# Grouping the output stores of an attention-times-value kernel in pairs, and putting SyncE's relay words into a register loop

## Chip, cores, metric

One core of one Trainium2 chip. The metric is the device time of one execution in microseconds (us). All runs told here were undisturbed ("fast"), so they are compared directly. "Ratio" is the mean time of one kernel's fast runs over that of the other's fast runs of the same rounds on the same chip, so it is not quite the ratio of the medians that are quoted.

In the profile's lines PE is TensorE's matrix multiply and PEld its weight load, DVE is VectorE, ACT ScalarE, POOL GpSimd and SP SyncE; a q behind a name means the engine's sequencer. HBM is the memory off the core, SBUF the one on it, and PSUM (in "banks") takes PE's results. A landing is the moment at which a transfer by DMA is complete.

## The reference

```python
batch, n_heads, seq, head_dim = 8, 12, 1024, 64
# attn_weights: (8, 12, 1024, 1024) float32;  v: (8, 12, 1024, 64) float32
out = np.einsum('bhqs,bhsd->bhqd', attn_weights, v).astype(np.float32)
```

The weights are 402.65 MB, v and the output 25.17 MB each.

## The kernel before

The 96 heads are taken in 24 quads of four heads; a quad is two units of 8.39 MB of weights. GpSimd loads each unit (float32 in HBM, bf16 in SBUF) into one of two buffers. PE transposes a unit's 16 groups, which frees its buffer, and multiplies with v; VectorE and ScalarE empty PSUM; ScalarE writes results to `osb`, a ring of ten quad slots, from which they are stored.

GpSimd's steady program: when the transposes of unit n are done, the load of unit n + 2 is issued; ahead of it, at odd quads, the next v load; behind it, at even quads, one store of eight heads (2.10 MB).

```python
for n in range(NU - 2):                      # NU = 48 units, NV = 24 quads
    q, i = n // 2, n % 2
    if i == 0 and q % 2 == 1 and q + 1 < NV:
        ...                                  # waits for the old v's last use
        load_v((q + 1) // 2)
    pool.wait_ge(s_t[True], (n + 1) * PER_DVE)
    load_attn(n + 2)
    if i == 0 and q % 2 == 0 and 0 < q <= HELD_FROM:    # HELD_FROM = 16
        store_2(q - 2)
for q in range(HELD_FROM, BY_SYNC, 2):       # held back to the end: quads 16 to 19
    store_2(q)
```

SyncE turns DMA completions into words (semaphore increments) for the engines: `s_half` for each landed unit, `s_vr` for each v, `s_free` for each stored pair of slots. PE waits for `s_half` at the ninth of a unit's 16 groups; ScalarE waits for `s_free` before it writes a slot again.

```python
for n in range(-2, NU - 2):                  # straight-line, one wait and one increment each
    if n + 2 < HALVED:
        nc.sync.wait_ge(s_abf[n % 2], 16 * ((n + 2) // 2 + 1))
    else:
        nc.sync.wait_ge(s_second[n + 2], 16)
    nc.sync.sem_inc(s_half)
    if n >= 0 and n % 2 == 0:
        q = n // 2
        if q % 2 == 1 and q + 1 < NV:
            nc.sync.wait_ge(s_v, 16 * ((q + 1) // 2))
            nc.sync.sem_inc(s_vr, 2)
        if q % 2 == 1 and 1 < q <= HELD_FROM:
            nc.sync.wait_ge(s_osb[(q - 3) // 2 % 2], 16 * ((q - 3) // 4 + 1))
            nc.sync.sem_inc(s_free)
# ... then the last stores, issued by SyncE
```

Of the kernel before, what the change touches and what calls it, by code (L numbers as in the profile page):

```python
# [10 lines left out]
def kernel(  # L11
# [18 lines left out]
    nc = tc.nc  # L30
# [15 lines left out]
    VB = S // VP // SB  # L46
    NV = NH // VH
    NU = 2 * NV


    HELD_FROM = NV - 8
# [4 lines left out]

    HALVED = NU - 2

    def slot(q):
        return q % NO  # L60
# [20 lines left out]
    with tc.tile_critical(no_gpsimd_drain=True):  # L81
# [18 lines left out]
        s_abf = [sem(f"s_abf{i}") for i in range(2)]  # L100
        s_second = {n: sem(f"s_second{n}") for n in range(HALVED, NU)}
        s_v0, s_v = sem("s_v0"), sem("s_v")
        s_osb = [sem(f"s_osb{i}") for i in range(2)]
# [13 lines left out]
        s_memset, s_const, s_vr = sem("s_memset"), sem("s_const"), sem("s_vr")  # L117

        s_half, s_free = sem("s_half"), sem("s_free")
# [33 lines left out]
        def transpose_back(parts=((0, 4, px[0]), (4, 4, px[1]))):  # L153
            for j0, jn, ps in parts:
                for j in range(jn):
                    last = pe.matmul(  # L156
                        out=ps[:, ds(j * P, P)],
                        lhsT=ot[:, j0 + j],
                        rhs=ident,
                        is_transpose=True,  # L160
                        start=(j == 0),
                        stop=(j == jn - 1),
                    )
                last.then_inc(s_back)
# [16 lines left out]
        def wait_both(s, n):  # L181
            for x in s:
                pe.wait_ge(x, n)

        def pe_unit(i, n, loaded, it):

            pe.wait_ge(*loaded)
            for g in range(G):
                if g == GH:
                    pe.wait_ge(s_half, n)  # L190
                transpose_g(abf[i], g, n)
            wait_both(s_ot, n)
            if i == 0:
                pe.wait_ge(s_vr, it)
                odd = pe.snap((it - 1) % 2)
                with pe.If(odd > 0):
                    spread_v(1, po + px)
                with pe.Else():
                    spread_v(0, po + px)
                wait_both(s_vbf, it * 2)  # L200
            transpose_back()
            wait_both(s_last, n)
            for hp in range(2):
                for h in range(2):
                    for half in range(2):
                        outs = po[hp][ds(half * D, D), ds(h * GH * VP, GH * VP)]
                        last = multiply(outs, 2 * hp + h, half)
                last.then_inc(s_m[hp])

        pe.wait_ge(s_const, 1 + VH)  # L210
        with nc.Fori(1, NV + 1, 1, engines=(PE,)) as it:
# [4 lines left out]
            pe_unit(1, second, (s_abf[1], loaded), it)  # L216
        wait_both(s_ot, NU + 1)
        transpose_back()


        def engine(dve):
# [11 lines left out]
            def back_copy(rows, j0, jn, ps, count):  # L233

                eng.wait_ge(s_back, count)
                return copy(  # L236
                    out=rows.rearrange("p (half j) d -> p j half d", half=2)[:, ds(j0, jn)],
                    in_=ps[:, ds(0, jn * P)].rearrange("p (j half d) -> p j half d", half=2, d=D),
                )
# [59 lines left out]
            rows = osb[:, slot(NV - 1), ds(G, G)]  # L299
            back_copy(rows, 4 * k, 4, px[k], 2 * NU + k + 1).then_inc(s_fin[k])  # L300

# [13 lines left out]
        def load_attn(n):  # L315
            pieces = [(0, G)] if n < HALVED else [(0, GH), (GH, GH)]
            for g0, gn in pieces:
                pool.dma_start(  # L318
                    out=abf[n % 2][:, ds(g0, gn)].rearrange("p g s -> p (g s)"),
                    in_=attn_q[n // 2][:, ds((n % 2 * G + g0) * S, gn * S)],  # L320
                ).then_inc(s_abf[n % 2] if g0 == 0 else s_second[n], 16)

        def load_v(iv):
            pool.dma_start(  # L324
                out=vr.rearrange("p two b x -> p two (b x)"), in_=v_2[iv]
            ).then_inc(s_v, 16)

        def store(q, fours, eng, done):
            eng.wait_ge(s_out, 2 * (q + fours) + 1)
            at_slot = osb[:, ds(slot(q), fours)].rearrange("p n r d -> p n (r d)")  # L330
            eng.dma_start(  # L331
                out=out_2[q // 2] if fours == 2 else out_q[q],
                in_=at_slot if fours == 2 else at_slot[:, 0],
                **({"single_packet": True} if eng is pool else {}),
            ).then_inc(done, 16)

        def store_2(q):
            store(q, 2, pool, s_osb[q // 2 % 2] if q < HELD_FROM else s_held)
# [14 lines left out]
        for h in range(VH):  # L353
# [9 lines left out]
            ).then_inc(s_const)  # L363
        for n in range(NU - 2):
            q, i = n // 2, n % 2
            if i == 0 and q % 2 == 1 and q + 1 < NV:
                for s in s_sp:
                    pool.wait_ge(s, 2 * q + 2)
                load_v((q + 1) // 2)
            pool.wait_ge(s_t[True], (n + 1) * PER_DVE)  # L370
            load_attn(n + 2)
            if i == 0 and q % 2 == 0 and 0 < q <= HELD_FROM:
                store_2(q - 2)
        for q in range(HELD_FROM, BY_SYNC, 2):
            store_2(q)
# [9 lines left out]
                out=v32_2[ds(p0, pn), two], in_=v_2[0][ds(p0, pn), two]  # L385
            ).then_inc(s_v0, 16)
        nc.sync.sem_inc(s_free, RING)
        for n in range(-2, NU - 2):

            if n + 2 < HALVED:  # L390
                nc.sync.wait_ge(s_abf[n % 2], 16 * ((n + 2) // 2 + 1))
            else:
                nc.sync.wait_ge(s_second[n + 2], 16)
            nc.sync.sem_inc(s_half)
            if n >= 0 and n % 2 == 0:
                q = n // 2
                if q % 2 == 1 and q + 1 < NV:
                    nc.sync.wait_ge(s_v, 16 * ((q + 1) // 2))
                    nc.sync.sem_inc(s_vr, 2)
                if q % 2 == 1 and 1 < q <= HELD_FROM:  # L400
                    nc.sync.wait_ge(s_osb[(q - 3) // 2 % 2], 16 * ((q - 3) // 4 + 1))
                    nc.sync.sem_inc(s_free)
        store(NV - 4, 2, nc.sync, s_end)
        store(NV - 2, 1, nc.sync, s_end)
        rows = osb[:, slot(NV - 1)].rearrange("p (u half j) d -> p u half j d", u=2, half=2)
# [41 lines left out]
```

## Time and profile before

| | before |
|---|---|
| median of the first 3 runs | 1054.85 us (1054.56 to 1054.9) |
| span of the profiled run | 1053.1 us |
| PE / ACT / DVE busy | 70 / 39 / 37% |
| share of the DMA engines, queue q0 | 99.1% |
| HBM traffic | 427.82 MB read, 25.17 MB written |

The row of the page that shows the stores one by one is the rate in 40 slices of 26 us, in GB/s, in the page's table of slices. It counts bytes on the SBUF side, where a load of weights is halved by the cast (4096 KB in the page's list of issues for the 8.39 MB of a unit) and a store is not (2048 KB, 2.10 MB), so a slice with a store in it stands out:

```profile
GB/s 235 224 217 218 218 244 219 219 214 249 231 214 251 215 219 258 217 219 230 243 217 210 259 217 218 259 219 219 248 217 217 218 211 225 219 208 230 206 216 339
```

The slices near 218 hold loads alone; those near 250 hold a store of 2.10 MB, and the last one is the burst of held stores.

### The profile page before, as it was taken

The numbers are of one execution on the slowest core, as the hardware profiler recorded it, in microseconds if no ns is written. First come the engines' busy times: TensorE is split into PE (matmuls) and PEld (weight loads), VectorE is DVE, ScalarE is ACT, GpSimd is POOL, SyncE is SP. The second block draws the span as 40 slices with busy tenths as digits, with TensorE's granted clock in tenths as the row PEclk, the third lists the DMA queues.
The fourth block names the chain that finished last, engine by engine and source line by source line (L and its number), as shares of the span: only waits on it lengthen the run. The fifth ranks groups of instructions, "written<-read, shape, count | busy, mean of one in ns | idle before, by whom it ended". The sixth has DMA issues, their size and how long they took to land.

```text
span 1053.1 us, 16530 instructions
## 1 busy us (share of the span) xinstructions
PE 738.0 (70%) x6920; PEld 692.4 (66%) x6920; DVE 388.8 (37%) x582; ACT 410.3 (39%) x493; POOL 45.1 (4%) x80
## 2 busy tenths in 40 slices
PE   0787677676697568667768757765776866875885
PEld 0686676565686567656668657765766866865874
DVE  0453343333353234333334324433333433532542
ACT  0354344433353334333335334433333533533542
POOL 1000000000000000000000000000000000000000
PEclk9989888898798888889879888888887987988998
DMA  9999999999999999999999999999999999999998
GB/s 235 224 217 218 218 244 219 219 214 249 231 214 251 215 219 258 217 219 230 243 217 210 259 217 218 259 219 219 248 217 217 218 211 225 219 208 230 206 216 339
DMA packets 14330, 240.19 MB, mean 228 GB/s; under 512 B 1269, under 2 KB 1781, under 8 KB 4725
## 3 DMA queue, kind: packets, MB, share of 16 engines
q0 software_dynamic: 12912, 233.84, 99.1%
q1 hardware_dynamic: 1413, 6.29, 1.5%
q8 instruction: 2, 0.03, 0.0%
q14 instruction: 3, 0.02, 0.0%
HBM read 427.82 MB, written 25.17 MB: 430 GB/s over the span
## 4 chain that ended last, share of the span: by engine, by line
DMA 75%; PE 22%; issue 1%; DVE 0%; SPq 0%; ACT 0%; POOL 0%; DVEq 0%
DMA abf<-in_attn_weights_dram 72%; PE bank L129 21%; DMA osb<-in_v_dram 3%; PE bank L171 1%; PE bank L156 0%; DVE vbf L229 0%; SPq L384 0%; PE bank L144 0%; DVE at L250 0%; DVE osb L236 0%; ACT ot L262 0%; POOL abf L318 0%; DVEq L249 0%; DVE vr L308 0%; DVEq L283 0%
## 5 line engine op out<-in xcount | busy, mean ns | idle before, releaser
L129 PE MATMUL bank<-ident,abf 128*128 128x128 f32 x3072 | 454.1, 318 | 273.6 <-DMA abf<-in_attn_weights_dram 264.4
L129 PEld LDWEIGHTS bank<-ident,abf 128*128 128x128 f32 x3072 | 444.2, 214 | 286.8 <-DMA abf<-in_attn_weights_dram 276.2
L250 DVE COPY at<-bank 128x1024 bf16<-128x1024 bf16 x480 | 320.4, 689 | 463.8 <-PE bank L129 460.0
L250 ACT COPY at<-bank 128x1024 bf16<-128x1024 bf16 x288 | 288.8, 1012 | 419.9 <-PE bank L129 419.9
L171 PE MATMUL bank<-at,vbf 128*64 128x256 bf16 x3072 | 215.0, 278 | 0.0
L171 PEld LDWEIGHTS bank<-at,vbf 128*64 128x64 bf16 x3072 | 196.8, 108 | 13.4 <-DVE at L250 4.0
L262 ACT COPY ot<-bank 128x512 f32<-128x512 f32 x48 | 28.1, 586 | 174.2 <-PE bank L171 174.2
L262 DVE COPY ot<-bank 128x512 f32<-128x512 f32 x48 | 33.2, 692 | 151.3 <-PE bank L171 151.3
L156 PE MATMUL bank<-ident,ot 128*128 128x128 f32 x392 | 52.2, 276 | 32.9 <-DVE vbf L229 32.1
L156 PEld LDWEIGHTS bank<-ident,ot 128*128 128x128 f32 x392 | 43.4, 141 | 45.0 <-DVE vbf L229 43.9
L236 ACT COPY osb<-bank 128x512 f32 (+1 forms) x97 | 52.2, 589 | 27.1 <-PE bank L156 26.3
L318 POOL DMA_DIRECT2D abf<-in_attn_weights_dram x50 | 27.3, 546 | 692.4 <-PE bank L129 691.4
L229 DVE CAST vbf<-bank 128x512 bf16<-128x512 f32 x48 | 30.9, 686 | 6.5 <-PE bank L144 6.5
L229 ACT CAST vbf<-bank 128x512 bf16<-128x512 f32 x48 | 25.8, 589 | 11.8 <-PE bank L144 11.8
L144 PE MATMUL bank<-vr,spread 32*128 32x512 bf16 x384 | 25.8, 377 | 0.0
L324 POOL DMA_DIRECT2D vr<-in_v_dram x11 | 7.8, 706 | 234.9 <-PE bank L144 234.9
L250 ACT ACT_TABLE_LOAD x12 | 15.4, 1283 | 1.3 <-SPq L81 1.1
L144 PEld LDWEIGHTS bank<-vr,spread 32*128 32x128 bf16 x384 | 10.2, 92 | 6.7
L308 DVE CAST vr<-osb 128x4096 bf16<-128x4096 f32 x1 | 2.3, 2294 | 30.4 <-DMA osb<-in_v_dram 30.4
L331 POOL DMA_DIRECT2D out_dram<-osb x10 | 7.2, 717 | 30.4 <-ACT osb L236 30.4
L355 POOL TENSOR_SCALAR_AFFINE_SELECT spread<-spread 32x512 bf16<-32x512 bf16 x4 | 2.5, 631 | 0.6
L236 DVE COPY osb<-bank 128x512 f32<-128x512 f32 x1 | 0.7, 692 | 3.1 <-PE bank L156 3.1
(8 smaller groups left out, 2.1 us busy)
## 6 DMA issues: line engine op xcount, KB each, us to landing
abf<-in_attn_weights_dram POOLq DMA_DIRECT2D x46, 4096.0 KB, 33.3
out_dram<-osb POOLq DMA_DIRECT2D x10, 2048.0 KB, 29.5
vr<-in_v_dram POOLq DMA_DIRECT2D x11, 1024.0 KB, 17.2
abf<-in_attn_weights_dram POOLq DMA_DIRECT2D x4, 2048.0 KB, 24.4
out_dram<-osb SPq DMA_DIRECT2D x1, 2048.0 KB, 13.7
osb<-in_v_dram SPq DMA_DIRECT2D x1, 1024.0 KB
out_dram<-osb SPq DMA_DIRECT2D x1, 1024.0 KB, 15.8
osb<-in_v_dram SPq DMA_DIRECT2D x1, 768.0 KB
```

What stands on the lines that cost most here:

```text
L129: last = pe.matmul(out=pt[g % 4][:, k], lhsT=words[:, k], rhs=ident, is_transpose=True, start=(k == 0), stop=(k == KW - 1),)
L144: last = pe.matmul(out=ps, lhsT=spread[rows, b], rhs=vr[rows, two, b], start=(b == 0), stop=(b == VB - 1),)
L156: last = pe.matmul(out=ps[:, ds(j * P, P)], lhsT=ot[:, j0 + j], rhs=ident, is_transpose=True, start=(j == 0), stop=(j == jn - 1),)
L171: last = pe.matmul(out=outs, lhsT=vbf[:, 2 * kw + par, h], rhs=at[:, ds(half * GH, GH), kw, ds(h * VP, VP), par], start=(n == 0), stop=(n ...
L229: copy(out=vbf[:, :, h], in_=ps.rearrange("p (k d) -> p k d", k=SB)).then_inc(s_vbf[e])
L236: return copy(out=rows.rearrange("p (half j) d -> p j half d", half=2)[:, ds(j0, jn)], in_=ps[:, ds(0, jn * P)].rearrange("p (j half d) -> ...
L250: ins = copy(out=at[:, g].rearrange("c k j two -> c (k j two)"), in_=bank[g % 4].bitcast(bf16),)
L262: copy(out=ot.rearrange("c j (h p) -> c h j p", h=VH)[:, ds(2 * e, 2)], in_=po[e].rearrange("c (h j p) -> c h j p", h=2, j=GH),).then_inc( ...
L318: pool.dma_start(out=abf[n % 2][:, ds(g0, gn)].rearrange("p g s -> p (g s)"), in_=attn_q[n // 2][:, ds((n % 2 * G + g0) * S, gn * S)],).th ...
L324: pool.dma_start(out=vr.rearrange("p two b x -> p two (b x)"), in_=v_2[iv]).then_inc(s_v, 16)
L331: eng.dma_start(out=out_2[q // 2] if fours == 2 else out_q[q], in_=at_slot if fours == 2 else at_slot[:, 0], **({"single_packet": True} if ...
L355: pool.affine_select(out=spread[ds(h * VP, VP)], in_=spread[ds(h * VP, VP)], compare_op=mybir.AluOpType.not_equal, fill=1.0, base=0, patte ...
```

## The change

The intent: fewer turns between loading and storing, by issuing two stores of eight heads together at every sixteenth head, and a shorter program for SyncE, by a register loop whose turn covers sixteen heads.

```diff
-            if i == 0 and q % 2 == 0 and 0 < q <= HELD_FROM:
+            if i == 0 and q % 4 == 0 and 0 < q <= HELD_FROM:
+                store_2(q - 4)
                 store_2(q - 2)
...
-        for n in range(-2, NU - 2):
-            (the straight-line words, shown above)
+        def relay(to, of, n, by=1):
+            nc.sync.wait_ge(of, n)
+            nc.sync.sem_inc(to, by)
+        def relays_of(four, eight, stored):
+            for n in range(4):
+                relay(s_half, s_abf[n % 2], four + 16 * (2 + n // 2))
+                if n == 2:
+                    relay(s_vr, s_v, eight + 16, 2)
+                    if stored is not None:
+                        nc.sync.wait_ge(s_osb[0], stored)
+                        relay(s_free, s_osb[1], stored, 2)
+        for i in range(2):
+            relay(s_half, s_abf[i], 16)
+        for t in range(2):
+            relays_of(32 * t, 16 * t, None)
+        with nc.Fori(1, HELD_FROM // 4 + 1, 1, engines=(mybir.EngineType.SP,)) as it:
+            stored = nc.sync.snap(it * 16)
+            for k in range(2):
+                four, eight = (nc.sync.snap(it * (2 * x) + k * x) for x in (32, 16))
+                relays_of(four, eight, stored if k == 0 else None)
+        for t in range(HELD_FROM // 2 + 2, NV // 2 - 1):
+            relays_of(32 * t, 16 * t, None)
+        for n in range(HALVED, NU):
+            relay(s_half, s_second[n], 16)
```

(The dots and the bracketed line mark cuts.)

More of the change, by code (lines that the diff above doesn't have):

```diff
@@ L387 @@
         nc.sync.sem_inc(s_free, RING)
-        for n in range(-2, NU - 2):
-            if n + 2 < HALVED:
-                nc.sync.wait_ge(s_abf[n % 2], 16 * ((n + 2) // 2 + 1))
-            else:
-                nc.sync.wait_ge(s_second[n + 2], 16)
-            nc.sync.sem_inc(s_half)
-            if n >= 0 and n % 2 == 0:
-                q = n // 2
-                if q % 2 == 1 and q + 1 < NV:
-                    nc.sync.wait_ge(s_v, 16 * ((q + 1) // 2))
-                    nc.sync.sem_inc(s_vr, 2)
-                if q % 2 == 1 and 1 < q <= HELD_FROM:
-                    nc.sync.wait_ge(s_osb[(q - 3) // 2 % 2], 16 * ((q - 3) // 4 + 1))
-                    nc.sync.sem_inc(s_free)
+        def relay(to, of, n, by=1):
[22 more added lines that the diff above has]
+            relay(s_half, s_second[n], 16)
         store(NV - 4, 2, nc.sync, s_end)
```

## The prediction

> **What bounds the kernel now.** I read the page's header and its table of slices first, then the queues and the bytes, then the chain of work that ended last in order of time, then a table of four stretches, and last the waits of GpSimd and SyncE.
>
> ```profile
> PE 738.0 (70%) x6920; PEld 692.4 (66%) x6920; DVE 388.8 (37%) x582; ACT 410.3 (39%) x493; POOL 45.1 (4%) x80
> DMA  9999999999999999999999999999999999999998
> q0 software_dynamic: 12912, 233.84, 99.1%
> q1 hardware_dynamic: 1413, 6.29, 1.5%
> q8 instruction: 2, 0.03, 0.0%
> q14 instruction: 3, 0.02, 0.0%
> HBM read 427.82 MB, written 25.17 MB: 430 GB/s over the span
> ```
>
> No compute engine is above 70%, while the 16 DMA engines are full in every slice. HBM traffic, 427.82 + 25.17 = 452.99 MB, is just the inputs (402.65 MB of weights, 25.17 of v) and the output (25.17), each once. So no byte can be saved. Instruction fetches on q8 and q14 are five packets in all.
>
> The chain of waits in order of time gives the pace of the stream. Its columns are start, length and what; every PE row is the start of an odd half-quad's transposes, the moment its load has landed, so two neighbouring PE starts are two loads of 8.39 MB apart, plus what lay between them in the queue:
>
> ```profile
> 436.30 10.42 PE bank L129 x64
> ...
> 479.81 8.03 PE bank L129 x64
> ...
> 523.35 9.67 PE bank L129 x64
> ...
> 566.89 9.46 PE bank L129 x64
> ...
> 828.58 8.03 PE bank L129 x64
> 836.61 0.28 issue
> 836.89 30.29 DMA abf<-in_attn_weights_dram
> 867.23 9.49 PE bank L129 x64
> ```
>
> The table of stretches (columns: length, then PE, weight load, DVE, ACT and POOL busy, PE clock, DMA share, GB/s counted at the SBUF side) has a period with one store, one with one v load, and one with neither:
>
> ```profile
> 479.81:523.35 43.54, 29.61 (x288) 27.74 (x288) 15.94 (x24) 16.41 (x20) 1.81 (x3) 0.89 1.00 237
> 523.35:566.89 43.54, 30.94 (x288) 29.06 (x288) 15.94 (x24) 17.72 (x21) 1.78 (x3) 0.84 1.03 220
> 828.58:867.23 38.65, 29.38 (x289) 27.50 (x289) 15.94 (x24) 16.41 (x20) 1.79 (x3) 0.91 0.98 210
> ```
>
> The bare period moves 16.78 MB in 38.65 us: 434 GB/s. A store of eight heads (2.10 MB) adds 43.54 - 38.65 = 4.89 us, which is 429 GB/s; a v load of the same HBM bytes adds the same 4.89 us. So a store costs its bytes and nearly nothing else. The chain itself calls only 72% DMA on the weights and 21% PE, because it goes from a landing back to the issue and from there to the transposes that freed the buffer. That is not what paces the stream: an issue joins a queue that still holds the other buffer's load.
>
> ```profile
> POOL abf L318 <- PE bank L129: 691.4, 35, 37.4
> POOL out_dram L331 <- ACT osb L236: 30.4, 8, 3.8
> SPq L394 <- DMA abf<-in_attn_weights_dram: 1025.7, 48, 25.2
> ```
>
> GpSimd waits 3.8 us before each of the eight stores, after the load has been issued. SyncE spends 1025.7 of 1053.1 us waiting for loads.
>
> [...]
>
> **The change part by part.** (1) Stores. GpSimd issued eight stores of eight heads in the steady part, one every second quad (a quad is four heads, two loads): at quads 2, 4, ... 16, each behind a load. Now it issues none at quads 2, 6, 10, 14 and two at 4, 8, 12, 16. The count stays at eight, the bytes too, and the shape (256 rows of 8 KB) too. First-order cost: 8 x 4.89 = 39.1 us before and after, difference 0. A period holding a pair should become 38.65 + 2 x 4.89 = 48.4 us and its counterpart without one 38.65; two such together are 87.1, the same as 2 x 43.54.
>
> What could be gained is a cost of switching between loads and a store. I bound it by the chain: the eight periods with a store (130.23 to 174.51, 218.05 to 262.02 and so on) last 44.28, 43.97, 43.64, 43.59, 43.54, 43.73, 43.83 and 43.57 us, mean 43.77; those with a v load 43.50 to 43.54, mean 43.52. The excess is 0.25 us each, 2.0 us in total. It is uneven, and the least of them has 0.02, so it need not belong to the stores. If all of it went with the switch, half the switches would save 1.0 us. I give this one chance in two: -0.5 us.
>
> The first store of a pair finds its rows written long ago, so GpSimd no longer waits 3.8 us before it; the second still does. That wait lay behind an issued load and is worth 0. Issuing the two takes 2 x 0.71 us of GpSimd, against over 10 us until it is wanted again. 0.
>
> (2) Free slots. The ring has ten quad slots. A slot pair used to be handed back when the load after its store had landed, at quads 3, 5, ...; now two come at once at quads 5, 9, 13, 17. ScalarE's sixth turn (quads 10 and 11) needs the sixth word, its eighth (14 and 15) the eighth; these come at quads 5 and 9. There are about five quads, over 200 us, to spare. 0.
>
> (3) SyncE's words. Every landing is still followed by one wait and one increment, now with thresholds in registers, plus some register operations and a branch in four turns. PE asks for the word of a load only at its ninth group, halfway through transposes of 8 to 10 us, so some 4 us after landing. [...] Even if PE did wait, the stream would not: by the chain it frees a buffer and GpSimd issues 8 to 11 us after a landing, and the next load (38.65 / 2 = 19.3 us) then still runs for about 9 us. [...]
>
> (4) Start and end. The first loads, the held stores of quads 16 to 19 and the last stores from SyncE are untouched. 452.99 MB at 434 GB/s are 1043.6 us of the 1053.1; the 9.5 us left are start, end and unevenness, outside the change. 0.
>
> Sum: 1054.85 - 0.5 - 0.05 = 1054.3 us.
>
> **The rivals.** *A dearer pair:* four megabytes of writes in a row could slow the memory or make a load late[...]. For it speaks only that no two stores are queued together before the very end. Against it: the issue that must not be late has 9 us to spare, growing by another store's 4.9 us, and at the end stores already run back to back. At 0.5 us for each pair this is +2 us, 1056.9.
>
> *Switching is what costs:* the whole 0.25 us excess goes with a switch, and perhaps the loads behind it become smoother: -1.0 to -2.0 us, 1052.9 to 1053.9. For it: only store periods have an excess above 0.02 us. Against: it does not repeat from one store to the next.
>
> *The register loop stalls SyncE:* [...] PE would then stand at its ninth group, and waits of PE for SyncE would appear. With 9 us of slack the time does not move; only a stall over 9 us each turn would give +1 to +10 us. I take it as very unlikely.
>
> *Nothing is to be had:* the store pieces are hidden work in a saturated stream and both parts are housekeeping: 1054.8.
>
> **Range and chances.** The runs before spread over 0.34 us. The rivals that I give weight reach from 1052.9 to 1056.9, the upper one with less. Predicted 1054.3 us, range 1052.9 to 1055.7 for 8 in 10. A 2% step is 21 us, more than ten times every term above: faster 0.01, same 0.98, slower 0.01.
>
> **What would show it.** Right: the same bytes, the DMA row full, the chain's periods cycling 48.4 / 43.5 / 38.65 / 43.5 us in the steady part with the same sum of about 174 us for eight loads, and GpSimd's waits before stores down from eight to four of 3.8 us. The switching cost: a pair's period below 48.4 + 0.25. A stalled SyncE: waits of PE or PEld on SyncE at line 129 beyond the two (5.4 us) there now at the halved loads. Wrong altogether: a slice with DMA below 9 in the steady part, GpSimd waiting at a DMA issue, ScalarE waiting for a free slot, or a bare period other than 38.6 us.

The sum, 1054.3 us, still counts a term of -0.05 us: it was the guess at what a shorter program for SyncE saves. The term that is left, the switching's, gives 1054.85 - 0.5 = 1054.35 us. A time for the bookkeeping of a loop's turn, also a guess, was never in the sum.

## The result, and the profile after

| | before | after |
|---|---|---|
| median of 6 runs each | 1054.8 us (1053.95 to 1055.22) | 1054.12 us (1053.7 to 1055.15) |
| ratio after / before | | 0.9996, 95% interval 0.9983 to 1.0009 |
| span of the profiled run | 1053.1 us | 1052.8 us |

The same time within noise. The medians differ by 0.7 us; the interval is 1.4 us wide to either side. The page of the changed kernel:

```profile
PE 727.1 (69%) x6920; PEld 681.4 (65%) x6920; DVE 388.3 (37%) x582; ACT 410.1 (39%) x493; POOL 44.9 (4%) x80
DMA  9999999999999999999999999999999999999998
GB/s 236 223 220 209 218 213 218 218 260 245 230 217 204 221 218 296 219 219 218 219 209 212 300 217 219 218 219 219 287 216 218 217 211 225 219 207 231 204 217 337
...
q0 software_dynamic: 12912, 233.84, 99.0%
...
q14 instruction: 2, 0.02, 0.0%
HBM read 427.82 MB, written 25.17 MB: 430 GB/s over the span
```

The stores did move: a single store's peak near 250 is gone, and four groups appear, the first cut by a slice's edge (260 and 245), then 296, 300 and 287. The bytes are the same and the DMA row is as full as before. The one other difference in the queues is an instruction packet on q14, 2 for 3. PE's 11 us less of busy time are no gain: PE is idle for loads anyway, and its waits for them rose from 264.4 to 278.2 us.

The stretches between PE's starts on odd units, the table that the prediction reads, for four neighbouring periods of the changed kernel (columns: length, busy time of PE, weight load, DVE, ACT and POOL, PE clock, DMA share, GB/s):

```profile
386.77:435.43 48.66, 29.37 (x288) 27.50 (x289) 15.94 (x24) 16.40 (x20) 1.81 (x3) 0.84 0.99 254
435.43:478.97 43.54, 32.12 (x288) 30.25 (x288) 16.13 (x24) 17.73 (x21) 1.07 (x2) 0.82 1.04 222
478.97:517.62 38.65, 29.39 (x288) 27.51 (x289) 15.94 (x24) 16.41 (x20) 1.78 (x3) 0.91 0.98 211
517.62:561.16 43.54, 29.74 (x288) 27.87 (x289) 15.94 (x24) 17.68 (x21) 2.48 (x4) 0.88 1.04 222
```

A period with a pair of stores, one with a v load, a bare one, one with a v load: 48.66, 43.54, 38.65, 43.54, together 174.39 us. Before, two store periods and two v periods took 2 x 43.54 + 2 x 43.54 = 174.2 us where the store periods were at their best. The time for a store has moved from one period into another, and that is all.

The waits, and SyncE's own:

```profile
POOL out_dram L332 <- ACT osb L237: 12.4, 4, 3.1
PE bank L130 <- SPq L393: 3.9, 2, 3.3
```

```profile
SPq L393 <- DMA abf<-in_attn_weights_dram: 1021.9, 48, 29.4
```

GpSimd now waits four times before a store instead of eight. PE waits for SyncE only at the two halved loads of the end, as before. SyncE itself does little but wait for loads.

### The profile page after: what moved, and what is told of

It reads as the page before. It is cut to its first block, busy times and chain, and to the rows that moved or that the text cites. A ratio compares the mean times of both kernels' runs of the same rounds, so it can differ in the third digit from the quotient of the medians.

```text
span 1052.8 us, 16564 instructions
## 1 busy us (share of the span) xinstructions
PE 727.1 (69%) x6920; PEld 681.4 (65%) x6920; DVE 388.3 (37%) x582; ACT 410.1 (39%) x493; POOL 44.9 (4%) x80
## 4 chain that ended last, share of the span: by engine, by line
DMA 76%; PE 21%; issue 1%; DVE 0%; SPq 0%; ACT 0%; POOL 0%; DVEq 0%
DMA abf<-in_attn_weights_dram 74%; PE bank L130 20%; DMA osb<-in_v_dram 3%; PE bank L172 1%; PE bank L157 0%; DVE vbf L230 0%; SPq L386 0%; PE bank L145 0%; DVE at L251 0%; DVE osb L237 0%; ACT ot L263 0%; POOL abf L319 0%; DVEq L250 0%; DVE vr L309 0%; DVEq L284 0%
## 5 line engine op out<-in xcount | busy, mean ns | idle before, releaser
L130 PE MATMUL bank<-ident,abf 128*128 128x128 f32 x3072 | 443.3, 314 | 283.6 <-DMA abf<-in_attn_weights_dram 278.2
L130 PEld LDWEIGHTS bank<-ident,abf 128*128 128x128 f32 x3072 | 433.4, 214 | 296.8 <-DMA abf<-in_attn_weights_dram 290.1
L263 ACT COPY ot<-bank 128x512 f32<-128x512 f32 x48 | 28.1, 586 | 174.2 <-PE bank L172 174.2
```

The source lines that it names most:

```text
L130: last = pe.matmul(out=pt[g % 4][:, k], lhsT=words[:, k], rhs=ident, is_transpose=True, start=(k == 0), stop=(k == KW - 1),)
L263: copy(out=ot.rearrange("c j (h p) -> c h j p", h=VH)[:, ds(2 * e, 2)], in_=po[e].rearrange("c (h j p) -> c h j p", h=2, j=GH),).then_inc( ...
```

## The experiments

The theory: the DMA stream is full from start to end, a store costs its bytes wherever it stands, and SyncE's words have slack. The rivals: a switch between loads and stores costs, so that grouping pays; or the register loop stalls SyncE. Two lengths are used for all runs. The **stream** is the time from the landing of unit 3 to that of unit 45, and the **end** that from the landing of unit 47, the last, to the end of the span. They come from the trace's landing records (one for each of the 16 DMA engines; the landing is the last of them). Landings and PE's starts agree within about 0.05 us in the steady part.

### The two kernels again

No edit.

> The kernel before, unedited, for a second trace. Theory (a saturated stream, the grouping of stores is worth nothing): ratio 1.000, and the uneven excess of the store periods (0.02 to 0.77 us in the first trace) falls on other periods or vanishes, as it is no property of the stores. Rival (a switch between loads and a store costs): the eight store periods again exceed the v-load periods by about 0.25 us in the mean, largest at the first ones.

> The changed kernel, unedited. Theory: ratio to before 0.9995 to 1.0005, a difference below 0.5 us. Rival (switching cost saved): 0.998 to 0.999, 1 to 2 us faster. In its first trace a period with a pair of stores lasted 48.7 to 48.8 us against 38.65 + 2 x 4.89 = 48.4; if that is the pair's own cost it repeats here.

Measured: before again 1054.62 us, ratio 1.000 (0.9986 to 1.0014); after again 1054.13 us, ratio 0.9995 (0.9981 to 1.0008). The chain of waits of the kernel before, second trace (start, length, what):

```profile
129.96 9.49 PE bank L129 x64
...
174.04 10.11 PE bank L129 x64
...
217.58 8.03 PE bank L129 x64
...
261.14 9.30 PE bank L129 x64
```

The store periods here are 44.08 (129.96 to 174.04) and 43.56 us (217.58 to 261.14); in the first trace the same two were 44.28 and 43.97. All eight of this trace have a mean of 43.75, against 43.77 in the first. So the rival's half of the expectation came true: the excess of some 0.2 us stays with the store periods and did not wander off to others. But its parts are scattered, from 0.02 to 0.54 us here. In the changed kernel the pair periods were 48.58 to 48.67 us in the second trace and 48.66 to 48.78 in the first, 0.15 to 0.35 above 38.65 + 2 x 4.89 = 48.43.

### Each half of the change alone

Paired stores with straight-line words:

```diff
-            if i == 0 and q % 2 == 0 and 0 < q <= HELD_FROM:
+            if i == 0 and q % 4 == 0 and 0 < q <= HELD_FROM:
+                store_2(q - 4)
                 store_2(q - 2)
...
-                if q % 2 == 1 and 1 < q <= HELD_FROM:
-                    nc.sync.wait_ge(s_osb[(q - 3) // 2 % 2], 16 * ((q - 3) // 4 + 1))
-                    nc.sync.sem_inc(s_free)
+                if q % 4 == 1 and 1 < q <= HELD_FROM + 1:
+                    for k in range(2):
+                        nc.sync.wait_ge(s_osb[k], 16 * (q // 4))
+                    nc.sync.sem_inc(s_free, 2)
```

> The paired stores alone, SyncE's words straight-line as before. Theory: ratio 0.9995 to 1.0005. Rival switching cost: as fast as the whole change, 0.998 to 0.999. Rival loop: if the register loop were what moved the time, this one stays at 1.000 and the loop alone moves.

The register loop with single stores (from the changed kernel):

```diff
-            if i == 0 and q % 4 == 0 and 0 < q <= HELD_FROM:
-                store_2(q - 4)
+            if i == 0 and q % 2 == 0 and 0 < q <= HELD_FROM:
                 store_2(q - 2)
...
-        with nc.Fori(1, HELD_FROM // 4 + 1, 1, engines=(mybir.EngineType.SP,)) as it:
-            stored = nc.sync.snap(it * 16)
+        with nc.Fori(1, HELD_FROM // 4, 1, engines=(mybir.EngineType.SP,)) as it:
+            stored = [(s_osb[1], nc.sync.snap(it * 16)), (s_osb[0], nc.sync.snap(it * 16 + 16))]
...
```

(The words of a turn are changed to match: one free slot pair at a time, and three turns instead of four.)

> The register loop alone (three turns), single stores as before. Theory: ratio 0.9995 to 1.0005, words sent within 0.1 us of the landing, no wait of PE on SyncE beyond the two at the halved loads. Rival[...]: waits of several us at line 129's PE rows in three turns, and 1.001 to 1.01.

Measured: pairs alone 1054.47 us, ratio 1.000 (0.9987 to 1.0014), with pair periods of 48.43 to 48.68 us; loop alone 1054.74 us, ratio 1.000 (0.9986 to 1.0013). The loop alone leaves this in the waits of PE, and this in the queues:

```profile
PE bank L130 <- SPq L392: 4.0, 2, 2.0
```

```profile
q14 instruction: 2, 0.02, 0.0%
```

Two waits, those of the halved loads: the loop stalls nobody. And the page answers which half removed the instruction packet: the loop. The five profiled kernels with this loop as it stands (the change twice, the loop alone and the two last experiments) have 2 packets on q14, the six with straight-line words have 3. These counts are of the span. In the trace of the loop alone an 8 KB packet begins 0.4 us after the span's end and another 1.3 us after it, where the straight-line kernels have just one, some 1.2 us after: there the packet slid past the end and was not saved. In both traces of the whole change it is gone. One packet of 8 KB, which took 0.31 us in the first trace of before, is the most that the shorter program bought.

### Larger and smaller groups

Four stores together at every 32nd head, and one store of four heads at every quad, both with straight-line words:

```diff
-            if i == 0 and q % 2 == 0 and 0 < q <= HELD_FROM:
-                store_2(q - 2)
+            if i == 0 and q % 8 == 0 and 0 < q <= HELD_FROM:      # fours
+                for x in (8, 6, 4, 2):
+                    store_2(q - x)
+            if i == 0 and 0 < q <= HELD_FROM:                      # or: halves
+                store(q - 1, 1, pool, s_osb[(q - 1) // 2 % 2])
```

(SyncE's thresholds for free slots are changed to match.)

> Four stores of eight heads back to back at every 32nd head (two groups in place of eight single stores), words straight-line. Theory: bytes alone count, ratio 0.9995 to 1.0005, a period with four stores lasts 38.65 + 4 x 4.89 = 58.2 us (up to 59 if each back-to-back store costs 0.1 us more, as the pairs seemed to). Rival switching cost: a quarter of the switches, 0.997 to 0.9985, 1.5 to 3 us faster.

> Sixteen stores of four heads, one per quad, in place of eight of eight heads: twice the switches, the same bytes. Theory: ratio 0.9995 to 1.001 (each period 38.65 + 2.45 = 41.1 us, plus the v load in every second one). Rival switching cost of 0.25 us or more each: 1.002, 2 us or more slower.

Measured: fours 1055.37 us, ratio 1.0004 (0.9991 to 1.0018); halves 1055.0 us, ratio 1.0003 (0.9989 to 1.0017). The stretch of the fours with the first group:

```profile
376.77:435.46 58.69, 29.80 (x288) 27.91 (x288) 15.99 (x24) 16.40 (x20) 1.81 (x3) 0.79 0.99 283
```

and two neighbouring stretches of the halves:

```profile
349.71:395.70 45.99, 31.38 (x288) 29.50 (x288) 16.04 (x24) 17.73 (x21) 1.60 (x3) 0.82 1.03 232
395.70:436.83 41.13, 31.74 (x288) 29.87 (x288) 16.13 (x24) 16.45 (x20) 2.32 (x4) 0.88 0.99 225
```

Four stores add 58.69 - 38.65 = 20.04 us, 5.01 each. A store of half the size and a v load add 45.99 - 38.65 = 7.34 us, just 4.89 + 4.89 / 2; in the next stretch a half-size store alone adds 2.48, against 2.45. So twice the switches cost no more, and a quarter of them save nothing that these runs resolve. The rival "a switch costs 0.25 us" wanted 1.5 to 3 us less for the fours and 2 us or more for the halves; neither came.

### No steady stores

The eight stores, SyncE's wait for each and the last wait for all of them are left out; SyncE hands the slots back unconditionally. The output of the first 16 quads is wrong.

```diff
-            if i == 0 and q % 2 == 0 and 0 < q <= HELD_FROM:
-                store_2(q - 2)
...
-                    nc.sync.wait_ge(s_osb[(q - 3) // 2 % 2], 16 * ((q - 3) // 4 + 1))
                     nc.sync.sem_inc(s_free)
```

> The eight steady stores left out; the output of the first 16 quads is wrong on purpose. Theory (a store costs its bytes in a full stream): 8 x 4.89 = 39.1 us less, 1015.7 us, ratio 0.963. Rival (stores partly hidden beside the loads): clearly less gain, for instance 20 us. Rival (stores cost their switches too): 41 us or more.

Measured: 1014.54 us, ratio 0.9617 (0.9602 to 0.9632); 40.2 us less than the 1054.72 of before in the same rounds, 5.02 us for each store. Two stretches:

```profile
296.63:335.26 38.63, 29.81 (x289) 27.94 (x289) 15.96 (x24) 16.41 (x20) 1.78 (x3) 0.91 0.97 208
335.26:378.80 43.54, 30.11 (x288) 28.25 (x289) 16.04 (x24) 17.67 (x21) 1.06 (x2) 0.84 1.05 225
```

Nothing of a store is hidden beside the loads: taking it away gives its whole time back. And with no store in the stream every period is 38.62 to 38.67 or 43.52 to 43.56 us, without a single one of the irregular longer ones. So the excess, 0.05 to 0.3 us for a store in the mean (table below), does belong to the stores, but by the halves and fours not to the number of switches.

### Late words

From the changed kernel, an idle count in SyncE between a load's landing and the word to PE:

```diff
             nc.sync.wait_ge(of, n)
+            if to is s_half:
+                with nc.Fori(0, 20, 1, engines=(mybir.EngineType.SP,)):     # 65 in the second
+                    nc.sync.sem_inc(s_idle)
             nc.sync.sem_inc(to, by)
```

> The changed kernel with about 6 us of idle counting in SyncE ahead of each word to PE. Theory (9 us of slack in the issue): PE waits about 2 us on SyncE in each of 46 more loads, and the time stays within 1 us, ratio 0.999 to 1.001. Rival (what PE waits goes to the end): 46 x 2 = 92 us slower, 1.09.

> The changed kernel with about 20 us of idle counting ahead of each word to PE, past the slack. Theory: a buffer is freed 20 + 4.5 us after its landing, a new load needs 21 us, so two loads take at least some 46 us: periods of 38.65 and 43.5 us grow to about 46, those with a pair of stores stay near 48.5 to 49. Sum 8 x 7.5 + 11 x 2.5, plus the last loads' words and the first: 80 to 130 us slower, DMA below 9 in some slices. Rival (slack much larger than I think): same time.

Measured with 20: 1055.53 us, ratio 1.001 (0.9995 to 1.0025). Measured with 65: 1282.57 us, ratio 1.2154 (1.2136 to 1.2173). The waits of PE with 20:

```profile
PE bank L131 <- DMA abf<-in_attn_weights_dram: 222.0, 45, 28.8
PE bank L131 <- SPq L397: 54.9, 39, 4.4
```

and with 65, the busy row of the DMA engines, and PE's wait:

```profile
DMA  9797697979977979979797997797997979779794
```

```profile
PE bank L131 <- SPq L397: 426.2, 48, 16.0
```

One turn of the count takes 0.31 us, so the first delay is about 6.2 us and the second 20.1. With the first, PE waits 54.9 us for SyncE, waits 56 us less for loads than in the changed kernel's trace (222.0 for 278.2), and the time is the same within noise: the slack is real, and this is how an engine's new wait looks when it costs nothing that the run times resolve. (In the trace the stream is 905.80 us and the end, where the last words are late too, 22.43.) With the second the slack is used up and the DMA row has holes. The size was mis-estimated, 228 us instead of 80 to 130. It is not that the delays queue behind one another: words come 20.07 to 21.03 us after their landing in the steady part, and only 9 of the 48 wait for the word before, 6.6 us in all. What the expectation had too short is the round of one buffer, 20 + 4.5 + 21, some 46 us. In the mean of units 4 to 43 the trace has 20.2 us from landing to word, 5.8 to the end of the transposes, 0.8 to the next issue and 25.2 from issue to landing, 52.0 us for two loads (43.1 in the changed kernel). The end grew too, to 38.10 us.

### The end, and the packets

From the changed kernel: three pairs and then two single stores; and stores without the single-packet request.

```diff
-            if i == 0 and q % 4 == 0 and 0 < q <= HELD_FROM:
-                store_2(q - 4)
-                store_2(q - 2)
+            if i == 0:
+                for x in {4: (0, 2), 8: (4, 6), 12: (8, 10), 14: (12,), 16: (14,)}.get(q, ()):
+                    store_2(x)
```

> The changed kernel with three pairs and then two single stores (at quads 14 and 16). In the traces so far the end, from the last load's landing, lasted 21.42 to 21.45 us with single, half or no stores in the steady part and 21.95 to 22.45 us with pairs or fours. If the last group's being a pair made that, the end is 21.45 us here and the time about 0.4 us below the changed kernel's; if not, 21.9 us or more and the same time. In either case within 1 us: ratio 0.999 to 1.001.

```diff
-                **({"single_packet": True} if eng is pool else {}),
```

> The changed kernel with GpSimd's stores not asked for as single packets. If the excess of a pair's period (48.4 to 48.8 us against 48.43) comes[...], it falls below 0.1 us here; if it is the writes themselves, it stays. Theory: ratio 0.9995 to 1.001 either way; rival (packets matter): 2 us or more slower[...].

Measured: last pair split 1054.19 us, ratio 0.9992 (0.9978 to 1.0006), end 21.77 us, between the two values that would have decided, so inconclusive. Plain packets 1054.17 us, ratio 0.9989 (0.9975 to 1.0003); its pair periods are 48.68 to 48.69 us, so the excess of 0.25 us for a pair does not come of the single-packet request, and nothing became 2 us slower without it.

All traces but those of the late words in one table; the excess is the stream less that of the kernel without stores and 8 x 4.89 us (865.45 + 39.12 = 904.57):

| kernel | groups x stores | stream us | excess us | end us |
|---|---|---|---|---|
| before, before again, loop alone | 8 x 1 | 906.23, 906.22, 906.96 | 1.7, 1.7, 2.4 | 21.45, 21.45, 21.43 |
| after, after again, pairs alone, plain packets | 4 x 2 | 905.64, 905.35, 904.94, 905.57 | 1.1, 0.8, 0.4, 1.0 | 21.95, 21.95, 22.16, 21.95 |
| last pair split | 3 x 2 + 2 x 1 | 905.27 | 0.7 | 21.77 |
| fours | 2 x 4 | 905.77 | 1.2 | 22.45 |
| halves | 16 x half | 905.80 | 1.2 | 21.45 |
| no stores | 0 | 865.45 | | 21.42 |

With pairs the stream is 1.1 us shorter in the mean (905.38 for 906.47) and the end 0.6 us longer (22.00 for 21.44), 0.5 us in all. The two groups of traces do not overlap in either column, but each row is a few single traces, and no ratio of run times resolves the 0.5 us. The traces show where the end is longer. The last small store lands 19.78 to 19.82 us after the last load where the steady stores are single, halved or absent, and 20.11 to 20.32 us after it where they are grouped, though it is issued no later (12.06 to 13.55 us for 13.55 to 13.80). In pairs alone and fours there are another 0.4 to 0.5 us behind that landing, in one pause of SyncE (0.45 and 0.46 us between two of its records that are less than 0.1 us apart in the other traces); an instruction packet follows 0.64 us after the pause, but no run tests whether the two belong together. Why the last store lands later after grouped stores is open: the bytes left at the end are the same, and the kernel without stores has the short end too.

The excess of the halves is no cost of each switch either: 1.0 of its 1.2 us lies in the first period with a store (46.98 us, where the seven later ones with a v load have 45.99 to 46.01).

## Why the prediction was right or wrong

- **The bound.** Right, and shown by the removal: a store that is taken out gives back 5.02 us, where 4.89 was predicted. The difference, 1.1 us for eight stores, is of the size of the excess.
- **Which side the rate is of.** The 434 GB/s are counted at HBM; on the SBUF side the bare stretch moves 210 GB/s, because the load halves its bytes. The trace shows that the stream has one steady rate in HBM bytes, for loads with the cast and nearly so for stores (429) without it; it does not show which part of the path sets that rate. And the additive 4.89 us says nothing of transfers that different engines issue: GpSimd issues the loads and the steady stores alike, all on q0.
- **The stores' periods.** Right: the cycle 48.66, 43.54, 38.65, 43.54 was predicted as 48.4, 43.5, 38.65, 43.5.
- **The switching term, -0.5 us.** The number agrees with the 0.5 us between the traces by luck, for the reason did not hold. It gave even chances to an excess that goes with switches; the excess does belong to stores (none without them), but twice the switches had 1.2 us of it and half as many groups as the pairs had 1.2 us too. What it goes with is not found. The pairs did not save a known cost.
- **The end, 0.** Wrong by about 0.5 us in the traces, in the other direction, cause open. Its term was too small to move the time out of the range.
- **GpSimd's wait.** Four waits for eight, as predicted; but 3.1 us each instead of 3.8. The prediction missed that the first store's issue (0.71 us) now fills part of that wait: 3.8 - 0.7 = 3.1. Worth nothing, as it said.
- **Free slots.** Right: ScalarE has no wait for SyncE's slots in either trace.
- **SyncE's loop.** Right that it has slack, and the delay of 6.2 us shows it. The bookkeeping was put at 1 us a turn, a guess; the trace has eight register operations of 32 to 59 ns and a branch of 40 to 50 ns in a turn, with 0.06 to 0.09 us from one start to the next (0.16 to 0.18 after the branch), below 1 us, and most stand after a word, where SyncE has 19 us (38.65 / 2) to fill. The program is shorter, but SyncE runs more of it: 127 recorded instructions for 93. The packet that the term of -0.05 us stood for is the one that q14 lost within the span, 2 for 3. The prediction also overlooked that its own trace has loops: VectorE's 24 loop branches (records of 50 to 63 ns, the next instruction mostly 0.20 us after the branch's start) and ScalarE's 12 (40 to 50 ns, mostly 0.22 us) could have told what a branch takes in this program, and that those loops have no stall of several us.
- **The rivals.** A dearer pair: 0.0 to 0.35 us for each instead of 0.5, about what two single stores have (some 0.2 us each), and no loss over all. A stalled loop: no. Nothing to be had: this is what the run times say.

## What to carry to other kernels

When the DMA row is full in every slice and the HBM bytes are those of the inputs and outputs, expect what happened here: moving transfers about inside the stream moved time from one stretch to another (ratio 0.9996). Count bytes and the head and tail, not the waits. Test such a bound by leaving a transfer out: if its whole time comes back (here 5.02 us for a store of 4.89), nothing about it was hidden. Whether its place matters is a second question, which took the pairs, fours and halves to answer. A helper engine's latency is measured by delaying it on purpose: a new wait of 55 us that leaves the time within noise shows the slack better than any argument, and a delay longer than the slack shows where it ends.
